# An encoder block on one core: where the first weight sums run, and how the down projection's right-hand loads queue

## The chip, the cores and the metric

The kernel runs on one core of one Trainium2 chip. The metric is device time in microseconds (us) of one execution, as the median of several runs.

## The reference, cut to what matters

One layer of an encoder over 1024 tokens of width 1024, in float32: a parallel mixer (a convolution group beside grouped-query attention), a cross-attention into 256 memory tokens, and a gated MLP with a width-3 convolution between its two projections. Every sub-layer has an RMS norm ahead and one behind, and adds to the residual. The change touches the end of the cross-attention and the MLP:

```python
y = memory_cross_attention(h, mem_n, ...); x = x + rmsnorm(y, norm_mem_post)
h = rmsnorm(x, norm_ffn_pre)
u = dwconv_centred(einsum("bsd,df->bsf", h, w_up), ffn_dw, ffn_dw_b)   # 1024 -> 2 x 2816
gate, val = u[..., :2816], u[..., 2816:]
y = einsum("bsf,fd->bsd", gelu(gate) * val, w_down)                    # 2816 -> 1024
x = x + rmsnorm(y, norm_ffn_post)
```

## The kernel before

Every matrix product runs in three matmuls on rounded halves: each operand is split into a high part (a cast on ScalarE) and a low part (operand minus high part, one subtraction), and high times high, high times low and low times high are accumulated. Both projections of the MLP also use a two-by-two block scheme with seven products in place of eight, so sums and differences of blocks are formed first.

**Cross-attention output.** A loop over eight blocks `t` of 128 tokens: `cross_gemm(t)` multiplies on TensorE, `cross_norm(t)` takes two norms (square on ScalarE, reciprocal root on GpSimd, scaling and residual on VectorE; L621 to L624, then L725 to L727) and `cross_operands(t)` transposes the result (L82), copies it out (L740) and forms the up projection's right-hand operands b11, b21, t1, t2, t3, t4 and b22 with their splits (`b_sub` L713, `b_split` L709 and L710). Blocks 0 to 3 give b11 and b21, blocks 4 to 7 the rest. The difference t3 (L748) is formed on GpSimd.

**Up projection.** A loop over 22 pairs `fi` of 128 gate columns and 128 value columns. `up_first(fi)` loads the gate weights (wg), splits them and runs two products, with b11 and b21. `up_operands(fi)` loads the value weights (wv), forms the four weight sums s12 and s34 on GpSimd (L813 to L816) and splits them and half of wv (L781; the low parts on VectorE, those of wv on GpSimd). `up_finish(fi)` runs the other five products (t1, t2, b22, t3, t4), adds them on VectorE (L842), runs the convolution, GELU and gating, and stores the pair's activations o in DRAM (L869). The loop of cross blocks already issues `up_first` of the first two pairs at its last block (`UP_PRE` = 2); their wg loads are issued at block 6. Beside it `down_load`, `down_sums` and `down_store` prepare the block differences of the down weights.

**Down projection.** Seven products m1, m2, m6, m7, m5, m4, m3, each over `NH` = 11 steps `i`. A step takes a left operand (a block of `acts[i]`, loaded back from DRAM at L903 and by `acts_load`, L906 to L908) and a right operand that `right(name, i)` loads for two steps at a time (tile `st`, L924). `operands` casts both (L945) and subtracts (L935) into one `op` tile, and 12 matmuls per step follow (L91 to L93). The load of the right operand is staged by turns in pool `rawp` (3 buffers) for odd counts and `tmpp` (4 buffers) for even counts:

```python
nst[0] += 1
st = (tmp if nst[0] % 2 == 0 else raw)("st").rearrange("p (i n) -> p i n", i=2)
```

So of m1's six loads the first, third and fifth are raw tiles and the second, fourth and sixth tmp tiles. Some of them carry activation loads behind them: m1's third load those of steps 0 and 1, its fourth those of 2 and 3, its fifth 4 and 5, its sixth 6 and 7, and m2's first load those of 8 to 10.

**Order.** The order of every engine's and every queue's instructions is fixed at build time by a planner that simulates a time line: an instruction goes in when its inputs and its tile's buffer are there in that simulation, by priority, which is the order in the program; tiles of one pool get their buffers in the order in which the program asks. On the chip each queue then runs strictly in that order. `tc.issue_after(ins)` only forces an order on one engine or queue. `tc.high_priority()` lifts the priority of what it encloses. All loads and stores here are issued from SyncE's queue (SP). Pool `wp` has 7 buffers, pool `act` 15: the cross-attention's tiles and the operands of the up projection share the latter, so t1's low part and later operands get a buffer only when earlier tiles are done with.

## Time and profile before

| what | value |
|---|---|
| median of 3 runs (lowest to highest) | 1430.79 us (1429.89 to 1430.89) |
| the profiled execution | 1431.57 us |
| its span in the profile | 1429.8 us |
| TensorE matmul busy in the span | 1376.8 us (96%) |
| VectorE, ScalarE, GpSimd busy | 1099.9, 699.5, 527.1 us |
| mean granted TensorE clock | 0.988 of full speed |

The span begins at the first profiled instruction and ends at the last; 1.8 us of the execution lie around it. In the rows below PE is TensorE's matmul, PEld its weight load, DVE VectorE, ACT ScalarE, POOL GpSimd, SPq the queue of SyncE that issues the transfers. "x4" behind a row means that four instructions are merged in it; the duration is then that of all. Brackets hold the idle time ahead of an instruction and what ended it. Busy time of PE is modelled from matmul ends, so a matmul's stated length overlaps its neighbour's.

### The profile page before, as it was taken

How to read it: one execution, taken by the hardware profiler on the slowest of the kernel's cores; microseconds unless marked ns; L12 is line 12 of the kernel's file. 1: busy time of each engine (PE TensorE's matmuls, PEld its weight loads, DVE VectorE, ACT ScalarE, POOL GpSimd, SP SyncE). 2: the span in 40 equal slices, each digit the busy share in tenths (PEclk: the TensorE clock that was granted, in tenths of full speed). 3: DMA queues.
4: the chain of work that ended last, by engine and by line, in shares of the span. 5: the costliest groups of instructions: out<-in, count | busy, mean ns of one | idle time of the engine just before them, and what ended most of it. 6: DMA issues, size and time to landing. Idle time of an engine off the chain costs nothing.

```text
span 1429.8 us, 18873 instructions
## 1 busy us (share of the span) xinstructions
PE 1376.8 (96%) x7042; PEld 1164.9 (81%) x7042; DVE 1099.9 (77%) x1443; ACT 699.5 (49%) x1190; POOL 527.1 (37%) x505
## 2 busy tenths in 40 slices
PE   9999999889999999999997999999999997999997
PEld 7889987679898888888885788888888886888885
DVE  6699899799999433435449989898898998696576
ACT  7426653678888444334335444444434444354452
POOL 5538877801011433102126455555555540000002
PEclk9999999999999999999998999999999998999998
DMA  7417760000000433203222443334444449523326
GB/s 239 138 50 230 244 224 14 21 1 1 30 1 1 148 104 133 74 32 116 88 89 88 162 147 133 121 130 147 133 147 147 148 148 331 212 82 96 103 89 213
DMA packets 77228, 170.08 MB, mean 119 GB/s; under 512 B 10065, under 2 KB 32849, under 8 KB 77137
## 3 DMA queue, kind: packets, MB, share of 16 engines
q1 hardware_dynamic: 77136, 168.88, 35.5%
q8 instruction: 55, 0.90, 0.2%
q14 instruction: 37, 0.30, 0.1%
HBM read 124.82 MB, written 44.04 MB: 118 GB/s over the span
## 4 chain that ended last, share of the span: by engine, by line
PE 69%; DVE 4%; DMA 2%; ACT 1%; issue 1%; POOL 1%; SPq 0%; POOLq 0%; DVEq 0%; ACTq 0%
PE p L101 9%; PE p L99 9%; PE p L98 9%; PE yd L91 5%; PE yd L92 5%; PE yd L93 5%; PE y L99 4%; PE y L101 4%; PE y L98 4%; PE pPT L82 3%; PE sc L101 2%; PE sc L98 2%; PE sc L99 2%; PE sp L536 2%; PE po L567 2%; PE sp L537 2%
## 5 line engine op out<-in xcount | busy, mean ns | idle before, releaser
L305 DVE SCALAR_TENSOR_TENSOR cacc<-conv,col,cacc 128x1009 f32<-128x1009 f32 (+14 forms) x120 | 145.8, 1275 | 4.8 <-ACT cacc L253 4.5
L86 POOL TENSOR_SCALAR rt<-ss 128x1 f32<-128x1 f32 (+1 forms) x43 | 14.9, 346 | 364.9 <-DVE ss L935 238.8
L92 PE MATMUL yd<-op 128*128 128x512 f32 x308 | 120.8, 393 | 0.0
L93 PE MATMUL yd<-op 128*128 128x512 f32 x308 | 120.6, 392 | 0.0
L91 PE MATMUL yd<-op 128*128 128x512 f32 x308 | 101.1, 393 | 9.1 <-ACT op L945 9.1
L945 ACT CAST op<-acts 128x512 fp32r<-128x512 f32 x77 | 47.8, 623 | 109.9 <-PE yd L93 99.5
L781 POOL TENSOR_TENSOR a<-wg,a 128x512 fp32r<-128x512 f32 x44 | 68.4, 1576 | 62.3 <-ACT a L780 62.3
L935 DVE TENSOR_TENSOR op<-acts,op 128x512 fp32r<-128x512 f32 x77 | 52.8, 688 | 46.7 <-ACT op L945 46.6
L781 DVE TENSOR_TENSOR a<-s,a 128x512 fp32r<-128x512 f32 x88 | 87.8, 1037 | 0.0
L831 ACT ACTIVATE c<-u,col 128x1024 f32<-128x1024 f32 x44 | 53.2, 1209 | 66.5 <-DVE u L842 66.5
L557 DVE TENSOR_TENSOR PL<-pPT,PH 128x512 fp32r<-128x512 f32 x128 | 83.1, 680 | 2.3 <-ACT PH L556 1.3
L539 DVE TENSOR_REDUCE nm<-sp 128x1 f32<-128x1024 f32 x64 | 78.0, 1218 | 7.4 <-PE sp L537 6.9
L780 ACT CAST a<-s 128x512 fp32r<-128x512 f32 x88 | 50.2, 619 | 64.8 <-DVE o L868 50.0
L842 DVE TENSOR_TENSOR u<-p,u 128x512 f32<-128x512 f32 x110 | 75.1, 683 | 7.2 <-PE p L101 6.2
L542 ACT ACTIVATE P<-sp,nm 128x1024 f32<-128x1024 f32 x64 | 72.1, 1126 | 15.4 <-PE pPT L82 6.5
L832 DVE SCALAR_TENSOR_TENSOR c<-u,col,c 128x1023 f32<-128x1023 f32 x44 | 56.5, 1285 | 28.8 <-ACT c L831 28.8
L556 ACT CAST PH<-pPT 128x512 fp32r<-128x512 f32 x128 | 69.4, 594 | 14.1 <-PE pPT L82 13.6
L91 PEld LDWEIGHTS yd<-op 128*128 128x128 f32 x308 | 58.5, 190 | 21.6 <-ACT op L945 9.5
L781 POOL TENSOR_TENSOR a<-wv,a 128x512 fp32r<-128x512 f32 x22 | 33.4, 1517 | 114.0 <-ACT a L780 112.9
L92 PEld LDWEIGHTS yd<-op 128*128 128x128 f32 x308 | 58.4, 190 | 12.7 <-DVE op L935 0.4
L82 PE MATMUL pPT<-ident,P 128*128 128x128 f32 x512 | 67.9, 273 | 0.7 <-DVE PL L557 0.7
L93 PEld LDWEIGHTS yd<-op 128*128 128x128 f32 x308 | 58.4, 190 | 12.2
(343 smaller groups left out, 4378.8 us busy)
## 6 DMA issues: line engine op xcount, KB each, us to landing
wg<-in_w_up_dram SPq DMA_DIRECT2D x22, 512.0 KB, 4.6
wv<-in_w_up_dram SPq DMA_DIRECT2D x22, 512.0 KB, 4.4
wd<-in_w_down_dram SPq DMA_DIRECT2D x22, 512.0 KB, 5.5
T_d<-wd SPq DMA_DIRECT2D x22, 512.0 KB, 3.2
act_d<-o SPq DMA_DIRECT2D x22, 512.0 KB, 3.1
acts<-act_d SPq DMA_DIRECT2D x44, 256.0 KB, 6.4
st<-T_d SPq DMA_DIRECT2D x20, 512.0 KB, 3.7
wmkv_r<-in_w_mkv_dram SPq DMA_DIRECT2D x16, 512.0 KB, 4.2
```

The lines of the kernel that those rows point to most:

```text
L82: nc.tensor.transpose(out=out_, in_=in_, identity=ident)
L91: nc.tensor.matmul(out=ps, lhsT=sh, rhs=mh, start=first, stop=False)
L92: nc.tensor.matmul(out=ps, lhsT=sh, rhs=ml, start=False, stop=False)
L93: nc.tensor.matmul(out=ps, lhsT=sl, rhs=mh, start=False, stop=last)
L98: nc.tensor.matmul(out=p, lhsT=sh, rhs=mh, start=first, stop=False)
L99: nc.tensor.matmul(out=p, lhsT=sh, rhs=ml, start=False, stop=False)
L101: ins = nc.tensor.matmul(out=p, lhsT=sl, rhs=mh, start=False, stop=last)
L305: nc.vector.scalar_tensor_tensor(out=acc[:, t0:t1_], in0=a[:, t0 + o:t1_ + o], scalar=cc(C_DW + c * 31 + j), in1=acc[:, t0:t1_], op0=ALU.m ...
L539: nc.vector.reduce_max(out=nm, in_=sp, axis=AX.X, negate=True)
L557: nc.vector.tensor_tensor(out=PL[dst], in0=p3, in1=f(PH[dst]), op=ALU.subtract)
L781: return eng.tensor_tensor(out=dst[:, 1, :], in0=src, in1=f(dst[:, 0, :]), op=ALU.subtract)
L842: return nc.vector.tensor_tensor(out=dst, in0=other if swap else ps, in1=ps if swap else other, op=op)
```

## The change

The down projection's right-hand loads are each queued behind the load before (the first behind the last load of up weights), and the first three are staged in raw tiles. The first pair's up weights are loaded at cross block 3 and its four sums formed there, on GpSimd. The second pair's weights go, at block 7, into one tile `gv` of pool `wp`, and its sums are formed on VectorE behind the last split of the right-hand operands. Block 7's t3 difference is formed on VectorE, and block 7's `cross_norm` has high priority.

```diff
     def b_split(name, ts_):
...
-        nc.vector.tensor_tensor(out=lo[:, :, ts_], in0=src[:, :, ts_], in1=f(hi[:, :, ts_]), op=ALU.subtract)
+        last_lo[0] = nc.vector.tensor_tensor(out=lo[:, :, ts_], in0=src[:, :, ts_], in1=f(hi[:, :, ts_]), op=ALU.subtract)
...
     def cross_operands(t, j):
+        third = nc.gpsimd if t < 7 else nc.vector
...
-            b_sub("t3", "b22", "b12", ts_, nc.gpsimd)
+            b_sub("t3", "b22", "b12", ts_, third)
...
+    rvs, sums = {}, {}
+
+    def up_sums(fi, rg, eng=None):
+        eng = eng or nc.gpsimd
+        rv = rvs.pop(fi) if fi in rvs else load_raw(w_up[fi, 1], "wv")
+        s12, s34 = tmp("s12"), tmp("s34")
+        eng.tensor_tensor(out=s12[:, H0], in0=rv[:, H0], in1=rv[:, H1], op=ALU.add)
+        eng.tensor_tensor(out=s12[:, H1], in0=s12[:, H0], in1=rg[:, H0], op=ALU.subtract)
+        eng.tensor_tensor(out=s34[:, H0], in0=rg[:, H0], in1=rv[:, H0], op=ALU.subtract)
+        eng.tensor_tensor(out=s34[:, H1], in0=rg[:, H1], in1=s12[:, H1], op=ALU.subtract)
+        sums[fi] = rv, s12, s34
+
     def up_operands(fi):
         rg, u, q = firsts.pop(fi)
-        rv = load_raw(w_up[fi, 1], "wv")
-        s12, s34 = tmp("s12"), tmp("s34")
-        nc.gpsimd.tensor_tensor(out=s12[:, H0], in0=rv[:, H0], in1=rv[:, H1], op=ALU.add)
...
+        if fi not in sums:
+            up_sums(fi, rg)
+        rv, s12, s34 = sums.pop(fi)
...
     UP_PRE = 2
+    PRE_T = 3
     for t in range(8):
-        if t == 6:
-            for fi in range(UP_PRE):
-                rgs[fi] = load_raw(w_up[fi, 0], "wg")
-        j = cross_norm(t, *cross_gemm(t))
-        if t == 7:
+        if t == PRE_T:
+            rgs[0], rvs[0] = load_raw(w_up[0, 0], "wg"), load_raw(w_up[0, 1], "wv")
+        y, xr = cross_gemm(t)
+        if t < 7:
+            j = cross_norm(t, y, xr)
+            if t == PRE_T:
+                up_sums(0, rgs[0])
+        else:
+            gv = wp.tile([128, 2, 1024], F32, tag="w", name="gv")
+            rgs[1], rvs[1] = gv[:, 0], gv[:, 1]
+            for i in range(2):
+                last_load[0] = nc.sync.dma_start(out=gv[:, i], in_=w_up[1, i])
+            with tc.high_priority():
+                j = cross_norm(t, y, xr)
             for fi in range(UP_PRE):
                 up_first(fi)
         cross_operands(t, j)
...
                 down_store(fi - 2)
+            if fi == 1:
+                with tc.issue_after(last_lo[0].ins):
+                    up_sums(fi, firsts[fi][0], nc.vector)
             lo = up_operands(fi)
...
-            st = (tmp if nst[0] % 2 == 0 else raw)("st").rearrange("p (i n) -> p i n", i=2)
-            ld = nc.sync.dma_start(out=st[:, :n, :], in_=src[i:i + n, :, b, :].rearrange("i p n -> p i n"))
-            pair[0] = st
+            st = (raw if nst[0] % 2 or nst[0] == 2 else tmp)("st").rearrange("p (i n) -> p i n", i=2)
+            with tc.issue_after(last_load[0].ins):
+                ld = nc.sync.dma_start(out=st[:, :n, :], in_=src[i:i + n, :, b, :].rearrange("i p n -> p i n"))
+            pair[0], last_load[0] = st, ld
```

## Rows read from the trace of the kernel before

**Rows 1.** The page: busy time, share of the span and instructions of each engine.

```profile
PE 1376.8 (96%) x7042; PEld 1164.9 (81%) x7042; DVE 1099.9 (77%) x1443; ACT 699.5 (49%) x1190; POOL 527.1 (37%) x505
```

**Rows 2.** Windows: stretch, length, busy us per engine, granted clock, DMA share, GB/s.

```profile
756.40:769.30 12.90, 11.85 (x56) 9.76 (x56) 12.18 (x15) 7.38 (x15) 6.54 (x6) 1.00 0.08 31
769.30:799.00 29.70, 18.38 (x57) 13.13 (x56) 26.45 (x26) 14.25 (x26) 20.04 (x14) 0.71 0.30 95
800.00:1195.00 395.00, 395.00 (x1742) 326.72 (x1743) 358.69 (x427) 165.89 (x228) 200.13 (x139) 1.00 0.45 149
1197.40:1202.90 5.50, 5.50 (x26) 4.35 (x24) 5.42 (x7) 3.85 (x5) 0.00 (x0) 1.00 1.02 381
1202.90:1217.40 14.50, 5.42 (x13) 4.14 (x13) 7.50 (x10) 4.08 (x8) 0.00 (x0) 0.65 1.02 370
1217.40:1238.00 20.60, 20.60 (x92) 17.02 (x91) 9.83 (x18) 6.92 (x13) 0.00 (x0) 0.99 0.70 253
```

**Rows 3.** Waits, 755 to 800 us: who for whom, us in total, times, longest.

```profile
PE p L99 <- DVE t3l L710: 3.8, 1, 3.8
...
PE p L98 <- ACT t1h L709: 3.1, 1, 3.1
```

**Rows 4.** Timeline of PE behind the last cross block.

```profile
757.45 1.06 PE L82 MATMUL pTs<-ident,h 128*128 128x128 f32 x8 [1.06 <-DVE h L727]
```

**Rows 5.** Timeline of DVE, 740 to 800 us.

```profile
740.03 1.28 DVE L727 SCALAR_TENSOR_TENSOR h<-x,rs,gG 128x1024 f32<-128x1024 f32 x1 [2.19 <-POOL rs L87]
...
762.84 1.83 DVE L710 TENSOR_TENSOR b22l<-r_b,b22h 128x512 fp32r<-128x512 f32 x1
...
766.29 1.21 DVE L624 TENSOR_TENSOR x<-x,x1r 128x1024 f32<-128x1024 f32 x1
...
773.91 1.34 DVE L713 TENSOR_TENSOR r_b<-r_b,r_b 128x512 f32<-128x512 f32 x1 [1.60 <-ACT r_b L740]
...
783.21 5.73 DVE L710 TENSOR_TENSOR t3l<-r_b,t3h 128x512 fp32r<-128x512 f32 x4
...
793.03 2.50 DVE L710 TENSOR_TENSOR t4l<-r_b,t4h 128x512 fp32r<-128x512 f32 x4
...
799.07 0.69 DVE L842 TENSOR_TENSOR u<-p,u 128x512 f32<-128x512 f32 x1 [1.13 <-PE p L101]
```

**Rows 6.** Timeline of ACT: the last norm's first step for cross block 5.

```profile
732.93 1.02 ACT L621 ACTIVATE x<-y 128x1024 f32<-128x1024 f32 x1 [5.93 <-issue]
```

**Rows 7.** Timeline of POOL: first and last of the second pair's four sums.

```profile
783.56 1.49 POOL L813 TENSOR_TENSOR s<-wv 128x512 f32<-128x512 f32 x1 [0.93 <-issue]
...
790.16 1.62 POOL L816 TENSOR_TENSOR s<-wg,s 128x512 f32<-128x512 f32 x1
```

**Rows 8.** One tile's instructions, 735 to 800 us: duration ns min/median/max.

```profile
L710 DVE TENSOR_TENSOR t1l<-r_b,t1h x4: 686/1764/1782, 748.6 to 776.9; 128x512 fp32r<-128x512 f32 x4
```

**Rows 9.** Waits, 1195 to 1240 us.

```profile
PE yd L91 <- ACT op L945: 9.1, 1, 9.1
ACT op L945 <- DMA st<-in_w_down_dram: 4.5, 2, 3.5
```

**Rows 10.** Timeline of SPq: m1's and m2's right-hand loads.

```profile
1159.33 0.39 SPq L924 DMA_DIRECT2D st<-in_w_down_dram  x1
...
1174.84 0.38 SPq L924 DMA_DIRECT2D st<-in_w_down_dram  x1
...
1179.53 0.38 SPq L924 DMA_DIRECT2D st<-in_w_down_dram  x1
...
1205.33 1.14 SPq L924 DMA_DIRECT2D st<-in_w_down_dram  x2
```

**Rows 11.** Timeline of DVE: the last pair's gated product o.

```profile
1206.09 1.22 DVE L868 TENSOR_TENSOR o<-u,c 128x1024 f32<-128x1024 f32 x1
```

**Rows 12.** The page, DMA issues: count, KB each, us to landing.

```profile
acts<-act_d SPq DMA_DIRECT2D x44, 256.0 KB, 6.4
st<-T_d SPq DMA_DIRECT2D x20, 512.0 KB, 3.7
```

More of the change, by code (lines that the diff above doesn't have):

```diff
@@ L703, in encoder_block @@
     BO = {}
+    last_lo = [None]
     def b_split(name, ts_):
@@ L806, in up_first @@
         firsts[fi] = (rg, u, q)
+    rvs, sums = {}, {}
[8 more added lines that the diff above has]
+        sums[fi] = rv, s12, s34
     def up_operands(fi):
         rg, u, q = firsts.pop(fi)
-        rv = load_raw(w_up[fi, 1], "wv")
-        s12, s34 = tmp("s12"), tmp("s34")
-        nc.gpsimd.tensor_tensor(out=s12[:, H0], in0=rv[:, H0], in1=rv[:, H1], op=ALU.add)
-        nc.gpsimd.tensor_tensor(out=s12[:, H1], in0=s12[:, H0], in1=rg[:, H0], op=ALU.subtract)
-        nc.gpsimd.tensor_tensor(out=s34[:, H0], in0=rg[:, H0], in1=rv[:, H0], op=ALU.subtract)
-        nc.gpsimd.tensor_tensor(out=s34[:, H1], in0=rg[:, H1], in1=s12[:, H1], op=ALU.subtract)
+        if fi not in sums:
+            up_sums(fi, rg)
+        rv, s12, s34 = sums.pop(fi)
         a2, a3 = W([2, 2, 512], "a2"), W([2, 2, 512], "a3")
```

## The prediction, made before the changed kernel ran

> **What bounds the kernel now.** First the page's busy shares: TensorE is busy 96% of the span [rows 1], so the time can fall only where TensorE stands or runs slowly, and I looked for those places. Cutting the span into windows shows two near the change, and nothing between them: from 800 to 1195 us, the up projection's steady state, PE is busy 395.00 of 395 us at full clock [rows 2]. There 1742 matmuls took 395 us, 0.227 us each. A product or a down step is 12 matmuls, 2.72 us.
>
> The first place is 756.4 to 799.0 us, from the last cross-attention product to the fifth product of the first pair. PE waits there, by the waits view, for operands of the right-hand side: 3.8 us for t3's low part, 3.1 us for t1's high part [rows 3]. In 769.3 to 799.0 us it ran 57 matmuls, at 0.227 us 12.9 us of work in 29.7 us, with a mean clock of 0.71: a loss of 16.8 us, some of it waiting and some matmuls at 1.2 instead of 2.4 GHz. From 756.4 to 769.3 us another 1.05 us are idle [rows 2]. VectorE is the cause: it is busy 26.45 of those 29.7 us, beside 20.04 us of GpSimd [rows 2].
>
> The second place is 1202.9 to 1217.4 us, in m1. PE has run 24 matmuls, steps 0 and 1, and then waits 9.1 us for a cast, and that cast for a right-hand load [rows 9]. The stretch holds 13 matmuls, 2.95 us of work, in 14.5 us at a mean clock of 0.65: a loss of 11.55 us [rows 2]. The queue's timeline tells why [rows 10]. Loads at 1159.33, 1174.84 and 1179.53 us are m1's first, third and fifth (activation loads of steps 0 and 1, tied to the third, follow at once behind the second row). The even ones, in tmp tiles, come only at 1205.33 us, two in a row, just ahead of the last o, at 1206.09 us [rows 11]. Pool tmpp hands out its buffers in program order and the last o asks ahead of them, so the planner could not place them earlier. Step 2's operand was loaded last.
>
> Everything that could be won is 16.8 + 1.05 + 11.55 = 29.4 us.
>
> **Part 1, the down projection.** With loads 2 and 3 in raw tiles, the second moves into the place of the row at 1174.84 us and the third to that of 1179.53 us. Steps 2 to 5 then have their right operands some 20 us before PE needs them. The wait of 9.1 us goes, and with it the slow clock behind it: 11.55 us. What is late next is load 4 (step 6), the first in a tmp tile; I leave it at 1205.33 us, as the last o still asks first. Before, the load at 1205.33 us let its first matmul start 9.1 us after 1202.9, at 1212.0 us, 6.7 us after the issue [rows 9, 10]. Step 6 is due at 1197.4 + 6 x 2.72 = 1213.7 us, so it is in time by 1.7 us.
>
> Behind load 4 now stands all that is ordered behind it: loads 5 and 6 and the activation loads of steps 2 to 10. Transfers run at 370 to 381 GB/s in this stretch with a DMA share above 1 [rows 2], so bytes set their time. Up to m2's first pair they are 18 activation blocks of 256 KB and 512 + 512 + 256 + 512 KB [rows 12], 6.5 MB, 17.4 us: landed by about 1223 us, due at 1197.4 + 11 x 2.72 = 1227.3 us. Nine more blocks and m2's second pair, 2.9 MB, take 7.7 us more: 1230.5 us, with 0.69 us for a subtraction [rows 8] and about as much for the cast 1231.9, due at 1232.7. The margin is so thin that I take 1 us off (between 0 and 3). Part 1 gives 10.5 us, between 8 and 11.55.
>
> Strict order costs nothing later: from m6 on the loads take turns between the pools in program order as before.
>
> **Part 2, the up projection's start.** Step by step, from the end of the last product at 757.45 - 1.06 = 756.4 us [rows 4].
>
> (a) Block 7's norm. Before, the residual addition L624 began at 766.29 us behind two subtractions for earlier operands of 1.8 us each [rows 5]; high priority puts the norm first. Block 5, undisturbed, took from 732.93 us (first square) [rows 6] to 740.03 + 1.28 us (end of L727) [rows 5], 8.4 us. Block 7's square can start at about 757.5 us: its tile comes free when block 6's norm ends, which the transposes at 757.45 us had waited for [rows 4]. So 757.5 + 8.4 + 1.06 for eight transposes [rows 4] + some 0.4 for the copy's head start, 767.3 us, against 773.91 us for the first difference before [rows 5]: 6.6 us earlier.
>
> (b) From there to the last split of t4. Before: 773.91 to 795.5 us, 21.6 us [rows 5]. The four t4 subtractions show the pace alone, 2.50 us for 4, about 0.6 each [rows 5]; t1's show 0.69 alone and 1.76 beside GpSimd [rows 8]. The work now is t1, t2, t3 and t4's differences (t3 new on VectorE, 0.6 us), splits of t1, b22 and t2 for block 7, four each of t3 and t4: 15 operations, 9.0 us. Four low parts of the first pair (2.4) and the two that the norm displaced (1.2) make 12.6 us. GpSimd keeps two splits of wv in this time, each costing VectorE 1.76 - 0.69 = 1.07 us: 14.7 us, ended at 782.0 us instead of 795.5. If all contention stayed, 21.6 us, at 788.9; with none, 779.9.
>
> (c) The second pair's sums. On GpSimd they filled 783.56 to 791.8 us, with another split between [rows 7]. On VectorE they are 4 x 0.6 = 2.4 us, ahead of the first additions that empty PSUM. Those start at 784.4 instead of 799.07 us [rows 5], 14.7 us earlier. The four products ahead (t1, t2, b22, t3; 10.9 us from 769.3) fit before, so this sets PE.
>
> (d) What is given back. The second pair's four low parts, done before 799.07 us till now, are still owed, 2.4 us. VectorE is busy 358.7 of 395 us in the steady state [rows 2], so it has 1.7 us a pair to catch up: I charge half, 1.2 us (0 to 2.4). PE still has idle pieces between 769.3 and 784.4 us, so a spell at 1.2 GHz can stay; the one in m1 cost 11.55 - 9.1 = 2.45 us. I charge 2.5 (0 to 2.5). Part 2 gives 14.7 - 1.2 - 2.5 = 11.0 us. Bounds: 7.8 - 2.4 - 2.5, about 3, and the whole 17.8.
>
> (e) At nothing: the first pair's sums at block 3. What hides them is a cross block's slack: PE needs 48 x 0.227 + 1.06 = 12.0 us for a block, and the norm's chain is over after 8.4. Four sums of about 1.6 us [rows 7] hold the chain by 6.4 us if all stand ahead of a reciprocal root on GpSimd, 2.8 more than the slack of 3.6; so 0 to 2.8 us if the cover is gone. They also hold two of four tmp and two of three raw tiles from block 3 on, so each block's tiles are those of the block before, free again after 8.4 us of 12.
>
> The Trainium skill ("Perfetto Trace Analysis", Optimizing Scalar/DVE Operations) says against (c) that GpSimd and VectorE share an SBUF read port, so that moving work between the two might not help. The trace agrees that they hinder each other [rows 8], yet by those rows four GpSimd sums cost VectorE 4.3 us in waiting against 2.4 us when it does them, and the first pair's go where VectorE has time. If moving brought nothing, the time would be that of the first rival.
>
> **Sum.** Against the profiled execution: 1431.57 - 10.5 - 11.0 = 1410.1 us. The runs' median lies 0.78 us below that execution, so 1409.3; I predict 1409.5 us. Under 0.2%, 2.9 us, counts as no change.
>
> **Rivals.** *VectorE stays the bound of the first place.* Contention stays: (b) ends at 788.9 us, additions start at 791.3, 7.8 us earlier, less 2.4 and 2.5 about 3 to 5 us; with part 1, 15 us, some 1416 us. For it: VectorE is busy 89% there [rows 2]. Against: eight sums and a difference leave GpSimd. *The wait in m1 moves to step 6.* Load 4 is held by the tmp buffer of an o whose store must land, and what is behind it is held too: PE stands 5 to 9 us at step 6, part 1 gives 2 to 6 us, about 1417 us. For it: the strict order lets nothing past. Against: buffers of the last pair's sums are long free. *No change worth the name*: both of these together, gain of some 3 us or less, 1428 us. *Slower:* the queue's hold at load 4 lasts on. It eats 11.55 us of part 1, 11 of part 2 and 2.9 more when step 6, due at 1213.7, waits 25.5 us (2.45 of them clock), so when load 4 is issued after about 1230 us by the old times, 24 us after the last o; then 1434 us or more. Against: nothing that holds a tmp buffer lasts so long.
>
> **Chances.** Forecast 0.56, its own range 1403 to 1416 (part 1 from 8 to 11.55, part 2 from 6 to 17). First rival 0.18, second 0.14, no change 0.05, slower 0.07. The range 1402 to 1420 takes in the forecast and most of the first two rivals. Faster by over 0.2% 0.88, within 0.2% 0.05, slower 0.07.
>
> **What would show it.** Right: no PE wait on a cast near 1190 us, seven in-order right-hand loads; block 7's L624 directly behind L623; t4's last split about 13 us earlier; PE's loss behind the cross blocks near 7 us; the steady state unchanged. Wrong: a PE wait at step 6 or at m2's start, VectorE operations still at 1.7 us beside GpSimd, a new wait for a buffer among cross blocks 4 to 7, or PE waiting for L842 in the first pairs.

## The result and the profile after

The changed kernel takes 1421.99 us (median of 5 runs, 1420.59 to 1424.29) against 1430.89 us for the kernel before on the same chip: a ratio of 0.9937, 95% interval 0.9924 to 0.9951. It is faster by 0.6%, 8.9 us, where 21.3 were forecast, and lies outside the range of 1402 to 1420 us.

The stages show where it went. They are cut by the start of TensorE's instructions in the trace. "14 products" runs from the end of the last cross-attention product to the 169th matmul of the up projection (two pairs of seven products of 12 matmuls); "first addition" is the time from that same end to VectorE's first addition that empties PSUM for the first pair (L842 before, L854 after). m1 ends with the start of its last matmul, m2 and "m6 to m3" begin at the start of the last matmul of the product ahead, so a wait for m2's first operand counts in m2. All in us, one profiled execution each:

```
kernel          first     14        rest    m1     m2     m6 to  tail   median   ratio to before,
                addition  products  of up                 m3             of runs  95% interval
before          42.67     60.11     380.97  41.61  29.92  150.30  10.48  1430.9   
after           38.77     56.14     380.80  29.69  34.27  152.12  11.05  1421.99  0.9937 0.9924-0.9951
down_only       43.33     60.73     380.96  29.69  34.27  152.12  11.37  1427.83  0.9976 0.9967-0.9986
up_only         37.52     54.89     380.80  41.06  29.92  150.29  10.17  1425.86  0.9963 0.9950-0.9976
act_store       38.65     56.04     380.80  29.69  34.31  152.09  11.05  1421.91  0.9934 0.9921-0.9947
m2_loads        36.66     54.01     380.80  29.69  32.40  152.75  11.05  1419.04  0.9917 0.9904-0.9931
no_order        37.48     54.87     380.80  31.67  29.92  150.32  10.16  1416.45  0.9898 0.9884-0.9911
order4          37.79     56.63     380.80  31.61  29.92  150.30  10.19  1418.45  0.9903 0.9885-0.9921
order_m1        35.69     53.15     381.60  29.69  34.26  152.14  10.18  1420.42  0.9920 0.9905-0.9934
splits_vec      38.27     57.11     380.80  29.69  34.26  152.14  11.06  1421.16  0.9928 0.9913-0.9943
operands_early  37.85     55.27     381.11  29.69  34.27  152.10  11.07  1422.19  0.9941 0.9927-0.9954
first1_behind   33.02     52.61     383.49  29.69  33.99  152.46  11.07  1420.37  0.9924 0.9908-0.9940
norm_clear      36.89     54.28     380.80  29.69  35.86  152.12  11.07  1421.20  0.9927 0.9913-0.9941
no_prio         38.78     56.15     380.80  29.69  34.27  152.14  11.07  1421.56  (one run)
finish_first    35.54     52.81     380.95  29.69  34.28  152.12  11.06  1419.31  0.9918 0.9905-0.9932
order4_finish   35.56     52.81     380.99  31.87  29.92  150.31  10.19  1414.53  0.9880 0.9864-0.9897
best2           34.86     52.42     380.97  31.80  29.92  150.31  10.19  1413.62  0.9882 0.9867-0.9898
```

By the first two lines m1 won 11.92 us, as forecast (11.55); then m2 gave back 4.35, the later products 1.82, and the tail 0.57. The up projection won 4.14 where 11.0 were forecast. Sum 9.32 us. The other 1.95 us of the two profiled spans' 11.3 arise ahead of these stages: the last cross product ended at 756.39 before and at 754.44 after. That is spread: in the other kernels of the table with that same code it ended anywhere between 754.3 and 759.1.

The up projection's stage spreads too. In eight kernels of the table (after, up_only, act_store, m2_loads, no_order, order4, order_m1, no_prio) every engine and the queue have the same instructions in the same order up to the end of the fourteen products. Their first addition came at 35.69 to 38.78 us, 37.67 in the mean, and the fourteen products took 53.15 to 56.63, 55.24 in the mean; the two kernels with the old code took 60.11 and 60.73. So 4.14 us is near the low end of what the change brings there; the mean of the traces says 5.2 and up_only's runs, below, 5.3.

The page after, its first line of shares (compare [rows 1]); VectorE and GpSimd are busy for about the same time as before:

```profile
span 1418.5 us, 18870 instructions
...
PE 1372.2 (97%) x7042; PEld 1161.3 (82%) x7042; DVE 1099.8 (78%) x1448; ACT 700.2 (49%) x1190; POOL 520.9 (37%) x500
```

The windows of the changed kernel: from the last cross product two pieces as long as the first two of [rows 2] (the second ends 4.0 us behind the first addition, in [rows 2] just ahead of it), the steady state, m1, m2, the later products:

```profile
754.40:767.40 13.00, 9.96 (x44) 7.96 (x44) 12.28 (x13) 7.64 (x14) 8.42 (x7) 0.92 0.29 95
767.40:797.20 29.80, 21.79 (x85) 16.79 (x84) 28.44 (x40) 14.85 (x27) 10.74 (x8) 0.86 0.18 59
797.20:1191.40 394.20, 394.20 (x1741) 326.40 (x1740) 357.54 (x425) 168.55 (x231) 196.31 (x136) 1.00 0.45 148
1191.40:1221.10 29.70, 29.70 (x133) 24.57 (x131) 18.62 (x27) 13.10 (x22) 0.00 (x0) 1.00 0.85 300
1221.10:1255.30 34.20, 31.01 (x133) 24.47 (x132) 31.35 (x53) 13.98 (x26) 0.00 (x0) 1.00 0.54 194
1255.30:1407.50 152.20, 150.97 (x662) 123.64 (x661) 107.25 (x179) 70.40 (x136) 10.24 (x13) 1.00 0.36 118
```

m1 now runs without a gap (29.70 of 29.70 us), but with a DMA share of 0.85 and 300 GB/s. m2's window holds 133 matmuls as m1's does and takes 34.20 us, beside a VectorE that is busy 31.35 of them. In the second piece GpSimd fell to 10.74 us, half of what it was, and VectorE went up to 28.44 of 29.80.

TensorE's waits of the changed kernel, first from 755 to 800 us, then from 1190 to 1410 us:

```profile
PE p L98 <- ACT t1h L711: 4.5, 1, 4.5
PE p L98 <- DVE u L854: 2.9, 1, 2.9
PE p L101 <- POOL a L784: 2.0, 1, 2.0
PE pTs L82 <- DVE h L729: 1.0, 1, 1.0
PE p L99 <- DVE t1l L712: 0.6, 1, 0.6
...
PE yd L91 <- ACT op L971: 3.0, 2, 1.8
PE yd L92 <- DVE op L961: 1.2, 2, 0.6
```

The 9.1 us in m1 [rows 9] are gone; its place take two waits of 1.8 and 1.2 us at m2's first and third step (1223.27 and 1230.60 us) and two of 0.6 in the product behind. At the start, t3's low part [rows 3] gave way to t1's high part and to the first addition.

The SP queue after: m1's six right-hand loads, the last store of an o, and m2's first two (the activation loads between are left out):

```profile
1153.24 0.38 SPq L950 DMA_DIRECT2D st<-in_w_down_dram  x1
...
1168.75 1.29 SPq L950 DMA_DIRECT2D st<-in_w_down_dram  x2
...
1189.01 1.21 SPq L950 DMA_DIRECT2D st<-in_w_down_dram  x1
...
1192.33 0.32 SPq L931 DMA_DIRECT2D acts<-act_d  x1
1201.61 0.32 SPq L881 DMA_DIRECT2D act_d<-o  x1
...
1203.63 0.38 SPq L950 DMA_DIRECT2D st<-in_w_down_dram  x1
...
1208.31 0.33 SPq L950 DMA_DIRECT2D st<-in_w_down_dram  x1
...
1213.78 0.38 SPq L950 DMA_DIRECT2D st<-in_w_down_dram  x1
...
1221.18 3.04 SPq L950 DMA_DIRECT2D st<-in_w_down_dram  x5
```

Loads 2 and 3 come at 1168.75 us and the fourth at 1189.01, so m1 has all it needs. Then the queue stands from 1192.65 to 1201.61 us, and m2's second load is issued at 1221.18 us, 29.8 us behind m1's first matmul, with nine activation loads between it and m2's first.

Last, block 7's norm on VectorE and GpSimd, with what stands between its steps (its first square, L621, started at 755.47 us):

```profile
756.67 1.69 POOL L86 TENSOR_SCALAR rt<-ss 128x1 f32<-128x1 f32 x1 [2.76 <-ACT x L621]
...
762.62 3.94 POOL L784 TENSOR_TENSOR a<-gv,a 128x512 fp32r<-128x512 f32 x2
766.65 0.52 POOL L86 TENSOR_SCALAR rt<-ss 128x1 f32<-128x1 f32 x1
...
759.02 1.28 DVE L623 SCALAR_TENSOR_TENSOR x<-y,rs,gG 128x1024 f32<-128x1024 f32 x1 [0.72 <-POOL rs L87]
760.23 0.68 DVE L715 TENSOR_TENSOR r_b<-r_b,r_b 128x512 f32<-128x512 f32 x1
760.82 0.68 DVE L712 TENSOR_TENSOR b22l<-r_b,b22h 128x512 fp32r<-128x512 f32 x1
761.42 2.32 DVE L624 TENSOR_TENSOR x<-x,x1r 128x1024 f32<-128x1024 f32 x1
...
768.84 1.27 DVE L729 SCALAR_TENSOR_TENSOR h<-x,rs,gG 128x1024 f32<-128x1024 f32 x1
...
774.88 2.01 DVE L715 TENSOR_TENSOR r_b<-r_b,r_b 128x512 f32<-128x512 f32 x2 [0.46 <-ACT r_b L743]
782.53 2.50 DVE L712 TENSOR_TENSOR t4l<-r_b,t4h 128x512 fp32r<-128x512 f32 x4
...
793.21 0.68 DVE L854 TENSOR_TENSOR u<-p,u 128x512 f32<-128x512 f32 x1
```

The norm takes from 755.47 to 770.1 us, 14.6 us, and not 8.4. Its first difference comes at 774.88 us, 20.4 us behind the last cross product; t4's last split ends at 785.0, and the first addition is at 793.21.

### The profile page after: what moved, and what is told of

It reads as the page before. It is cut to its first block, busy times and chain, and to the rows that moved or that the text cites. A ratio compares the mean times of both kernels' runs of the same rounds, so it can differ in the third digit from the quotient of the medians.

```text
span 1418.5 us, 18870 instructions
## 1 busy us (share of the span) xinstructions
PE 1372.2 (97%) x7042; PEld 1161.3 (82%) x7042; DVE 1099.8 (78%) x1448; ACT 700.2 (49%) x1190; POOL 520.9 (37%) x500
## 3 DMA queue, kind: packets, MB, share of 16 engines
q1 hardware_dynamic: 77136, 168.88, 35.9%
## 4 chain that ended last, share of the span: by engine, by line
PE 68%; DVE 4%; DMA 2%; ACT 2%; POOL 1%; issue 1%; SPq 0%; POOLq 0%; DVEq 0%; ACTq 0%
PE p L101 9%; PE p L98 9%; PE p L99 9%; PE y L99 4%; PE y L101 4%; PE y L98 4%; PE yd L92 3%; PE yd L93 3%; PE yd L91 3%; PE pPT L82 3%; PE sc L101 2%; PE sc L98 2%; PE sc L99 2%; PE sp L536 2%; PE po L567 2%; PE sp L537 2%
## 5 line engine op out<-in xcount | busy, mean ns | idle before, releaser
L86 POOL TENSOR_SCALAR rt<-ss 128x1 f32<-128x1 f32 (+1 forms) x43 | 15.5, 360 | 347.9 <-DVE ss L961 234.2
L92 PE MATMUL yd<-op 128*128 128x512 f32 x308 | 120.3, 391 | 1.3 <-DVE op L961 1.2
L93 PE MATMUL yd<-op 128*128 128x512 f32 x308 | 119.6, 389 | 0.0
L91 PE MATMUL yd<-op 128*128 128x512 f32 x308 | 97.7, 390 | 3.0 <-ACT op L971 3.0
L784 POOL TENSOR_TENSOR a<-wg,a 128x512 fp32r<-128x512 f32 x42 | 64.8, 1565 | 72.6 <-ACT a L783 72.6
L854 DVE TENSOR_TENSOR u<-p,u 128x512 f32<-128x512 f32 x110 | 75.1, 683 | 5.7 <-PE p L101 4.5
```

Of the source, the lines that this page charges most:

```text
L91: nc.tensor.matmul(out=ps, lhsT=sh, rhs=mh, start=first, stop=False)
L92: nc.tensor.matmul(out=ps, lhsT=sh, rhs=ml, start=False, stop=False)
L93: nc.tensor.matmul(out=ps, lhsT=sl, rhs=mh, start=False, stop=last)
L784: return eng.tensor_tensor(out=dst[:, 1, :], in0=src, in1=f(dst[:, 0, :]), op=ALU.subtract)
L854: return nc.vector.tensor_tensor(out=dst, in0=other if swap else ps, in1=ps if swap else other, op=op)
```

## The experiments

**The two halves alone.** down_only has the edit of `right()` and the parts above as before; up_only the reverse.

> Only the down projection's edit (order of the right-hand loads, first three in raw tiles); the up projection is that of before. First theory, the two parts add up and each is worth what the windows of the changed kernel show: down part 5.2 us, so about 1425.7 us against 1430.9 before, with the cast waits of m2's first steps (1.8 and 1.2 us) in the trace. Rival, the parts spoil each other: alone the down part gives the 10.5 us that were forecast, about 1420.4 us, with no wait at m2's start.

> Only the up projection's edits; the right-hand loads are staged and queued as before. First theory, the parts add: about 4.1 us, 1426.8 us, with the 9.1 us wait in m1 still there. Rival, the start of the up projection gives nothing at all and what looked like 4 us is the spread of executions (2.0 us of the changed execution's lead came about in code that is the same): 1430 to 1431 us.

Measured: 0.9976 and 0.9963, about 3.4 and 5.3 us; both together 9.0 us. So the halves add, and neither eats the other's gain. down_only has m1, m2 and the later products of the changed kernel to 0.01 us, up_only those of the kernel before to 0.6 us: what the down projection gave back comes from the edit of `right()` alone.

**act_store: the last o's store leaves the SP queue.** The queue stood in front of that store for 9 us; the idea is that on ScalarE's queue it holds nobody up.

```
-        nc.sync.dma_start(out=act_d[fi], in_=o)
+        (nc.scalar if fi == NF - 1 else nc.sync).dma_start(out=act_d[fi], in_=o)
```

> The changed kernel, but the last pair's o is stored from ScalarE's queue, so that SyncE's queue does not stand still from 1192.7 to 1201.6 us until o is there. Theory, the held queue makes the loads behind late: loads 5 and 6 and m2's first come 6 to 9 us earlier, the waits at m2's start (1.8 and 1.2 us) go, 3 to 4 us less than the changed kernel, about 1418 us. Rival, bytes: transfers run at 390 GB/s from 1210 to 1230 us anyway and m2's first loads stand behind 6 MB of activations: no change beyond 1 us, 1421 to 1423 us.

Measured: no change (0.9934; m2 34.31). The fifth load was issued at 1197.32 us, 5.3 us behind m1's start instead of 12.3, but the queue then stood from 1200.4 to 1206.83 us in front of an activation load. By the queue's own waits that load waited for the very store:

```profile
SPq L932 <- DMA act_d<-o: 7.0, 2, 6.4
```

So the queue was not freed of the last o: it stood until the store had landed (issued at 1202.2 us, landed at 1206.8), where in the changed kernel it stood until o was ready. The hold moved and m2 gained nothing. That the store's place alone makes m2 late falls; whether the hold does, this run does not test, but the runs on the order, below, do.

**m2_loads: the activation loads of steps 8 to 10 come behind m2's third load, not its first.**

```
-            behind = {..., "m2": range(8, NH) if i == 0 else ()}.get(name, ())
+            behind = {..., "m2": range(8, NH) if i == 4 else ()}.get(name, ())
```

> The six activation loads of steps 8 to 10 are ordered behind m2's third right-hand load instead of its first; nothing else is edited. Theory (the activation loads that stand in the queue ahead of m2's right-hand loads make these late, under the strict order): m2's second right-hand load is issued at about 1215 us instead of behind the activation loads, PE's two waits for m2's casts (1.81 and 1.23 us) fall below 1 us in all, m2's stretch goes from 34.27 to about 30 us, the products behind it keep 150.3 to 152.1, and the time falls by 4 to 5 us, to about 1417.5. Rival 1 (bytes: transfers there run at about 390 GB/s, so what is put back is late in its turn): PE then waits for left-hand casts of steps 8 to 10 or for the next product's loads, the down projection stays within 1.5 us of 216.1 us, and the time stays at 1421 to 1423. Rival 2 (VectorE is full behind m1, at 10.00 of 10 us): the waits move into the next products, m2 gets shorter and the rest longer by as much, time 1421 to 1422.

Measured: m2's second load at 1215.32 instead of 1221.18 us; m2 32.40 instead of 34.27, the later products 152.75 instead of 152.12. Of the 6.2 us 1.2 came back: the order behind m2's first load is a small part. What is put back is late in its turn, which is rival 1, and part of it moves into the next products, rival 2. (Its start was 2.1 us shorter in the profiled execution, with no edit there; that part of its lower time is not the edit's.)

**no_order: the staging tiles without the order.**

```
-            with tc.issue_after(last_load[0].ins):
-                ld = nc.sync.dma_start(...)
-            pair[0], last_load[0] = st, ld
+            ld = nc.sync.dma_start(...)
+            pair[0] = st
```

> The first three right-hand loads keep their raw tiles, but no load is ordered behind the one before; the rest of the change stays. Theory (the staging tiles take away m1's wait, and the strict order is what delays m2): m1 stays near 30 us, m2 goes back towards the 29.9 us that it took before, the later products to 150.3, and the time falls to 1416 to 1418. Rival 1 (the order is what keeps loads in time; without it the planner lets one of m1's later loads, of the tmp pool, slip behind others): a PE wait of 3 to 9 us in m1 as before, m1 at 33 to 42 us, time 1424 to 1428. Rival 2 (bytes alone): m1 and m2 as in the changed kernel, 1421 to 1423.

Measured: the theory's numbers. m2 29.92, the later products 150.32, m1 31.67 (one wait of 1.6 us at step 6), the tail 10.16; the ratio falls to 0.9898, its interval clear of the changed kernel's. Its windows of m1 and m2:

```profile
1191.00:1222.70 31.70, 30.06 (x132) 24.54 (x132) 22.96 (x36) 13.48 (x22) 0.00 (x0) 1.00 1.03 369
1222.70:1252.60 29.90, 29.90 (x133) 24.76 (x132) 29.63 (x51) 14.85 (x27) 0.00 (x0) 1.00 0.42 146
```

In m1's time the transfers run at 369 GB/s and not 300: over 29.7 us that is 2.0 MB more, the size of eight activation loads. So less is left for m2's time, in which the rate falls to 146. VectorE is as full in m2 as before (29.63 us), but not late.

**order4 and order_m1: which tie does it.** order4 keeps the order among the first four loads, order_m1 among all six of m1.

```
-            with tc.issue_after(last_load[0].ins):
+            with tc.issue_after(last_load[0].ins) if nst[0] <= 4 else ExitStack():       # order4
+            with tc.issue_after(last_load[0].ins) if name == "m1" else ExitStack():      # order_m1
```

> The order of the right-hand loads ends with the fourth: the second, third and fourth are still queued behind the one before, the fifth and all later ones are free. Theory (the tie of the fifth load, whose raw tile is free early, to the fourth, whose tmp tile waits for the last o, is what makes all later loads late): the fifth load is issued ahead of the last o's store, before 1197 us, m2's loads at about 1214 us as in the kernel without any order, m2 at 29.9 us, the later products at 150.3, m1 at 29.7 to 31.7, the down projection at 210 to 212 us, the time 1416 to 1417.5. Rival (it is the order among the first three that costs, or the bytes): the down projection stays at 216.1 us within 1 us and the time at 1421 to 1423.

> The six right-hand loads of m1 are queued one behind the other, the loads of the later products are free: the other half of the same question. Theory (the tie between the fourth and the fifth load does the harm): the loads come as in the changed kernel, m1 29.7, m2 34.3 and the later products 152.1 us, time 1421 to 1423. Rival (the ties within m2 and behind it do the harm): m2 goes back to 30 and the later products to 150.3 us, time 1415.5 to 1417.

Measured: order4 has m2 and the later products of the kernel without order (29.92, 150.30), order_m1 those of the changed kernel (34.26, 152.14). In m1 the two differ only in the ties of the fifth and the sixth load. order4's queue, its right-hand loads from 1190 us on (its m1 begins at 1194.6 us):

```profile
1190.87 0.39 SPq L950 DMA_DIRECT2D st<-in_w_down_dram  x1
...
1198.13 0.38 SPq L950 DMA_DIRECT2D st<-in_w_down_dram  x1
...
1205.34 0.38 SPq L950 DMA_DIRECT2D st<-in_w_down_dram  x1
...
1211.98 0.33 SPq L950 DMA_DIRECT2D st<-in_w_down_dram  x1
...
1217.22 2.77 SPq L950 DMA_DIRECT2D st<-in_w_down_dram  x4
```

The row at 1205.34 us is the fourth load: it is the one for step 6, whose wait ends at 1212.66 us. By their count two loads have passed it, and m2's other loads begin at 1217.22, 22.7 us behind m1's first matmul instead of 29.8. With the tie, the fifth load comes 12.3 us behind m1's start in the changed kernel, behind the last o's store. Without it, it comes 3.7 us ahead of m1's start, m2's first at 3.6 and the fourth at 10.8 us behind it; the activation loads tied to them come along and fill the time in which the queue of the changed kernel stands. The price of letting them pass is the 1.6 us at step 6.

**splits_vec: the second pair's two weight splits on VectorE**, so that GpSimd is free for block 7's second root.

```
-        a_split(a1[:, 0], rg[:, H0], nc.gpsimd)
+        a_split(a1[:, 0], rg[:, H0], nc.vector if fi == 1 else nc.gpsimd)     (and a1[:, 1] likewise)
```

> The changed kernel, but the low parts of the second pair's first operand (two subtractions from gv) run on VectorE, not GpSimd. Theory, GpSimd's queue holds block 7's norm: these two took 3.94 us ahead of its second reciprocal root, slowed the residual addition to 2.32 us and let PE wait 2.0 us; without them the first t1 difference comes 3 to 5 us earlier and the time is 1417 to 1419 us. Rival, VectorE's amount of work sets it: 1.2 us more on VectorE, 1422 to 1423 us.

Measured: the norm ended 1.6 us earlier, t4's last split 1.7, the first addition 0.5, and the time did not move (0.9928).

**operands_early: the first pair's operands traced ahead of the second pair's first products.** In the changed kernel four casts of the first pair stand on ScalarE from 769.59 us on, ahead of block 7's copies at 774.27, though their sums were long done.

```
-            for fi in range(UP_PRE):
-                up_first(fi)
+            up_first(0)
+            lo0 = up_operands(0)
+            up_first(1)
...
-            lo = up_operands(fi)
+            lo = up_operands(fi) if fi else lo0
```

> The first pair's weight operands are made ahead of the second pair's first product in program order, so that their two tiles come out of the pool first and their splits, which needed to wait for nothing, move ahead of block 7's copies on ScalarE and VectorE. Theory (in the changed kernel block 7's copies at 774.27 us stand behind four casts of the first pair from 769.59 us on, because the pool hands out buffers in program order): the copies come within about 1 us of the transposes at 771.2 us, the first difference at about 772 instead of 774.88 us, t4's last split and the first additions about 3 us earlier, the first fourteen products 53 instead of 56.14 us, the time 1418 to 1419. Rival 1 (VectorE's amount of work between 770 and 793 us sets the additions, whatever its order): the additions stay within 1 us of 793.2 us and the time within 1 us of 1422. Rival 2 (the casts now stand in front of block 7's norm): the norm's end moves later than 770.1 us, and the time is 1423 or more.

Measured: rival 1, and the later norm of rival 2 without its longer time. The norm ended 20.25 us behind the last cross product instead of 15.67, the first difference came at 22.5 instead of 20.4, the first addition yet at 37.85 instead of 38.77. The time stayed.

**first1_behind: the second pair's first two products traced behind block 7's operands.**

```
-            for fi in range(UP_PRE):
-                up_first(fi)
+            up_first(0)
         cross_operands(t, j)
+    up_first(1)
```

> The second pair's first two products are traced behind block 7's operands, so the transposes and copies of block 7 stand ahead of them on TensorE and ahead of the first pair's casts on ScalarE. Theory (the norm itself, 14.6 us long because GpSimd's two weight splits and block 6's work share its engines, sets the first difference; the copies come 4.2 us later still because of the casts): block 7's copies follow the norm's end at about 770 us within 2 us, the first difference comes at about 772 instead of 774.88 us, but TensorE, which has nothing else ready, waits some 4 us more for the transposes; the first fourteen products stay at 55 to 58 us, the time at 1421 to 1423. Rival (the copies behind the casts are the whole loss): no longer wait for the transposes than 1 us, the stretch at 52 to 53.5 us, the time 1418 to 1419.5.

Measured: the norm as long as before, the first difference 2.6 us earlier, a wait of 8.2 us for the transposes, as the theory has it; the fourteen products shorter (52.61, the rival's number) and the rest longer by 2.7 us. The up projection is at 436.1 us where the changed kernel has 436.9. Nothing won.

**norm_clear: block 7's norm with nothing between its steps.** Block 6's differences and splits and the second pair's weight splits are ordered behind it; block 6's third difference goes to VectorE too.

```
-            for fi in range(UP_PRE):
-                up_first(fi)
+            up_first(0)
+            with tc.issue_after(last_norm[0].ins):      # the instruction of L729
+                cross_differences(6)
+                up_first(1)
         cross_operands(t, j)                            # now without block 6's differences
```

> Block 6's differences and splits and the second pair's first weight splits are ordered behind block 7's norm, and block 6's third difference is VectorE's; so nothing of another block stands between the steps of block 7's norm. Theory (two waits in VectorE's queue, 1.2 and 1.04 us, one in GpSimd's, 1.66 us, and slower instructions beside GpSimd's splits, 2.3 us, made the norm 14.6 instead of 8.4 us from its first square to the end of its last instruction): the norm takes 8.4 to 10 us. What it brings is open: if the norm was what part 2 lacked, the first fourteen products take 51 to 53 instead of 56.14 us and the time is 1417 to 1419; if VectorE's amount of work counts (block 6's differences are still owed), the stretch stays at 55 to 57 us and the time at 1421 to 1423.

Measured: the norm took 10.7 us instead of 14.6 and ended 11.8 us behind the last cross product, much nearer to the forecast's step. Yet t4's last split ended at 29.90 instead of 30.58, and three of the eight kernels with the long norm (m2_loads, order4, order_m1) have it at 29.8. The first addition at 36.89 and the stretch of 54.28 lie inside the spread of those eight (35.69 to 38.78 and 53.15 to 56.63), and the time is not clearly below the changed kernel's. So 3.9 us at the norm bought 0.7 us at t4's last split at most, and nothing at the first addition that can be told. That m2 took 35.86 instead of 34.27 is not the edit's: the same two waits are there, and behind the first a spell at 1.2 GHz (granted clock 0.95 over m2, 1.00 in the changed kernel).

**no_prio: the norm without the block of high priority.**

> The block 'with high priority' around block 7's norm is taken off; nothing else. If the priority does nothing here: the same norm of 14.6 us from the first square to the end of the last instruction, and the same waits of TensorE (4.5, 2.9 and 2.0 us). If it does something: a longer norm, and a later first difference.

Measured: the same norm of 14.6 us, waits within 0.2 us, 1421.56 us. Its trace has the instructions of the changed kernel on every engine and on the queue, in the same order from start to end: the priority moved none.

**finish_first: the first pair's additions traced ahead of the second pair's operands.**

```
+        if fi == 0:                     # in up_finish, behind the fifth addition
+            down_sums(0, seventh)
...
+            if fi == 1:
+                down_load(1)
+                up_finish(0)            # five additions, then the wd differences
             lo = up_operands(fi)
-            down_load(fi)
-        if fi:
+            if fi != 1:
+                down_load(fi)
+        if fi > 1:
             up_finish(fi - 1)
-        else:
-            down_sums(0, lo)
```

> The first pair's additions, which empty PSUM, are traced ahead of the second pair's operand work, so VectorE does them behind the second pair's sums and four low parts and ahead of the weight differences of the down projection (which wait for a load until 789.2 us). Theory (VectorE's order between t4's last split at 785.0 us and the first addition at 793.21 us is what holds PE): the first addition comes at about 790.5 us, PE's wait of 2.9 us for it falls to about 0.5 us, the first fourteen products take about 54 instead of 56.14 us, the time 1419 to 1420. Rival 1 (the amount counts, and what is put off is late for the second pair): PE waits for the second pair's operands or later additions instead, the first fourteen products stay within 0.7 us of 56.14 us, time 1421 to 1423. Rival 2 (the products' order is what changes, as PE takes pair 0 later or earlier): the stretch is longer than 57 us.

Measured: the first addition 35.54 us behind the last cross product instead of 38.77, no wait for it, fourteen products in 52.81 instead of 56.14 us, ratio 0.9918 (its interval overlaps the changed kernel's). The theory holds: work which nobody was waiting for stood ahead of the additions. But the changed kernel's profile is at the slow end of the eight kernels with its instructions; against their means (37.67 and 55.24) the edit wins 2.1 and 2.4 us. It comes to the same in order4_finish and, with the cleared norm, best2 (52.81 and 52.42), all three below the lowest of the eight.

The timeline also tells where the eight differ. The third pair's first two weight splits start on GpSimd 34.6 to 35.7 us behind the last cross product, just as VectorE does the last of its list. Of VectorE's last two instructions ahead of the first addition both are then longer by 1.1 us (after, act_store, no_prio, order4), only the last (up_only, m2_loads, no_order), or none (order_m1). VectorE in the changed kernel, its neighbour on GpSimd, and VectorE in up_only:

```profile
789.51 0.68 DVE L784 TENSOR_TENSOR a<-s,a 128x512 fp32r<-128x512 f32 x1
790.11 1.51 DVE L776 TENSOR_TENSOR wd<-wd 128x256 f32<-128x256 f32 x1
791.54 1.74 DVE L784 TENSOR_TENSOR a<-s,a 128x512 fp32r<-128x512 f32 x1
...
790.04 2.70 POOL L784 TENSOR_TENSOR a<-wg,a 128x512 fp32r<-128x512 f32 x2 [14.50 <-ACT a L783]
```

```profile
789.77 0.42 DVE L776 TENSOR_TENSOR wd<-wd 128x256 f32<-128x256 f32 x1
790.11 1.77 DVE L784 TENSOR_TENSOR a<-s,a 128x512 fp32r<-128x512 f32 x1
```

In finish_first the additions run beside those splits at 0.68 us each, four in 2.73 us from 790.35 us on, and the two weight differences behind them took 2.81 us. The windows from the last cross product to the first addition, of the kernel before, the changed one, norm_clear and finish_first, in that order (the third pair of numbers is VectorE's):

```profile
756.40:799.10 42.70, 30.26 (x112) 22.89 (x112) 38.67 (x40) 21.64 (x40) 26.68 (x20) 0.80 0.24 76
```

```profile
754.40:793.20 38.80, 28.58 (x113) 22.26 (x112) 36.72 (x46) 22.05 (x40) 15.16 (x12) 0.87 0.24 77
```

```profile
755.70:792.60 36.90, 27.00 (x113) 21.24 (x112) 32.96 (x47) 21.73 (x40) 11.23 (x10) 0.86 0.24 81
```

```profile
754.80:790.30 35.50, 27.38 (x110) 21.60 (x110) 33.81 (x44) 21.57 (x40) 12.05 (x10) 0.86 0.26 84
```

VectorE is busy for 91, 95, 89 and 95% of each. Little in the first addition's way is a wait; it is a list of instructions, single ones longer beside GpSimd's, and its length is nearly the length of the stretch.

**order4_finish and best2: the good parts together**, the second with the cleared norm as well.

> The order that ends with the fourth load, and the first pair's additions ahead of the second pair's operand work. If the two edits are independent: up projection's first fourteen products at about 53 us, the down projection at 210 to 212 us, the time 1413 to 1415, which is 8 us below the changed kernel. If one takes away the other's gain (the additions moved ahead push the wd work and so the right-hand loads later): 1416 or more.

> The kernel with the order up to the fourth load and the first pair's additions ahead, and in addition the cleared norm. If the norm was what part 2 lacked: 2 to 4 us below that kernel's 1414.5, about 1411. If the amount of VectorE's work counts: 1414 to 1416.

Measured: 0.9880 and 0.9882, 1414.53 and 1413.62 us, against 1421.99 for the changed kernel. The two edits are independent (52.81 in the one place, 212.1 in the down projection). The cleared norm adds nothing that can be told on top. TensorE's waits that are left at the start in order4_finish; that for L854 is gone:

```profile
PE p L98 <- ACT t1h L711: 4.6, 1, 4.6
PE p L101 <- POOL a L784: 2.0, 1, 2.0
PE pTs L82 <- DVE h L729: 1.0, 1, 1.0
PE p L99 <- DVE t1l L712: 0.6, 1, 0.6
```

## Why the prediction was wrong

**Part 1, m1: right.** Loads 2 and 3 came some 20 us ahead of need, m1 fell by 11.92 us, the slow clock behind the wait went with it, and load 4 was in time.

**Part 1, m2: mis-sized.** The term "1 us off (between 0 and 3)" measured 4.35 in m2 and 1.82 in the products behind; with 0.57 of the tail, 6.7 us. The working let all that is queued behind load 4 run at 370 to 381 GB/s, the rate of the stretch before. Under the order the queue stood for 9 us in front of the last o's store, and m1's time passed at 300 GB/s. Counted from m1's start, m2's first two loads were issued at 22.4 and 29.8 us; by the trace they landed at 28.4 and 35.9, where the forecast had 25.6 and 33.1: 2.8 us late each, against margins of 4.3 and 0.8. The second is thereby late; the first is in time for TensorE by its landing, but its cast stood on ScalarE behind m1's four evictions (L1038, 1220.14 to 1222.2 us) and came at 1222.57. "Strict order costs nothing later" was wrong too: 1.8 us. The experiments on the order settle it: without it, or with it up to the fourth load, both prices vanish. The rival "the wait in m1 moves to step 6" had the right cause (the last o, and an order that lets nothing past) and the wrong place: the order brings load 4 early (1189.01 us), protects step 6, and charges m2.

**Part 2, (a) to (c): the steps failed as a chain.** In us from the end of the last cross product, forecast and measured: first difference 10.9 and 20.4; from there to t4's last split 14.7 and 10.1; from there to the first addition 2.4 and 8.2; sum 28.0 and 38.8 (up_only, with the same instructions, 37.5). The first and most expensive was (a), "high priority puts the norm first": it did nothing (no_prio), and the norm took 14.6 us. The timeline accounts for 6.1 of the 6.2 us above 8.4: two waits behind other work on VectorE (1.1 ahead of L624, 1.0 ahead of L729), one behind GpSimd's two weight splits (1.7), and two instructions longer than elsewhere (1.2 at the first L86, 1.1 at L624). The other 3.3 us of (a) lie behind the norm: block 7's copies stood behind casts on ScalarE until 774.27 us. But the norm was not the bound either: norm_clear ended it 3.9 us earlier, and the first addition stayed inside the spread of the kernels with the long norm. And (b) came out short for the same reason for which (a) came out long: the work was the same, in another order; the first pair's four low parts, which (b) charges, ran ahead of the first difference (from 770.24 us on). What the forecast should have summed is VectorE's list from the last cross product to the first addition, 38.67 us of 42.70 before. The change adds five instructions to it (four sums and a difference), its order two more (weight differences of the down projection, in the old kernel behind the addition), and it takes contention off: 38.67 became 36.72 us, and idle time fell from 4.0 to 2.1. In (c) four low parts and two pieces of the down projection's weight differences stood ahead of the additions too, where the forecast had the sums alone.

**What the first addition buys: forecast too low, (d).** In all kernels of the table but three (order4, splits_vec, first1_behind) the fourteen products end 17.25 to 17.56 us behind the first addition. From before to after it moved by 3.90 us and the stretch by 3.97; with finish_first by 7.13 and 7.30. So nothing was given back for clock or owed work; 3.7 us were charged.

**The rival "VectorE stays the bound"** is what happened, with less than its price: the additions came 3.9 us earlier (5.3 by the mean of the eight kernels against the two with the old code) and not 7.8. Its case "against", that eight sums and a difference leave GpSimd, is true of this stretch only (the first pair's four stay on GpSimd, at block 3) and was weighed wrongly, as five of the nine went onto the full engine. Both parts were short at once, by 5.3 (with the tail) and 6.9 us (5.8 by that mean), and a range built mostly on one rival at a time did not hold that.

**(e) at nothing: right**, as far as it shows: no new wait among cross blocks 4 to 7, and the last cross product's end, 756.4 and 756.9 us with the old code, lies amid the 754.3 to 759.1 with the new.

Of moving work between GpSimd and VectorE, on which the forecast quoted the Trainium skill ("Perfetto Trace Analysis", Optimizing Scalar/DVE Operations): the runs agree with it more than the forecast did. Here 46 instructions of VectorE took 36.72 us where 40 had taken 38.67, and in splits_vec 49 took 36.87; the moved instructions cost VectorE next to nothing, and won little.

Open: what makes GpSimd's splits fall on two, one or none of VectorE's last instructions ahead of the first addition when the program is the same; and why the order of the program, with the tie, has the fifth load and all behind it after the last o's store.

## What to carry to other kernels

Where one engine is busy above 90% of a stretch, don't forecast a chain of steps through it: sum the instructions that it must do between two fixed events, and move out of that list what nobody waits for; here this was worth some 2 us, and a norm shorter by 3.9 us nothing that could be told. A strict order of loads across two buffer pools lets none pass, and the bytes not moved while the queue stands are missing later, in a place that looks unrelated; tie only as far as the loads that were late.

## What the runs showed unexpectedly

- One kernel's runs spread by 2 to 5 us (order4: 1414.81 to 1419.64), and the profiled executions show where: with the same code, the last cross product ended between 754.3 and 759.1 us. In the same traces m1 took 29.69 us in each of eleven kernels. A change of 2 us is better read from a stage that repeats like this than from the time; the stage of the first addition, with its spread of 3.1 us, needs several traces.
- What slows VectorE beside GpSimd is not merely that both are busy: L624 took 2.32 us in the changed kernel, beside a subtraction of GpSimd's (L715) and the start of its weight splits, and 1.23 us in norm_clear, where those splits began 0.15 us behind it and ran on through it.
- A GpSimd instruction on a 128x1 tile (L86) took 1.69 us with VectorE busy throughout (756.67 us in the changed kernel) and 0.19 us in norm_clear while VectorE stood idle.
